# Expert loop with its tokens' rows loaded and turned inside the loop, 13 weight buffers, and two pairs' weights requested ahead of the router

## The chip, the cores and the metric

The kernel runs on one core of one Trainium2 chip. The metric is the device time of one execution in microseconds, taken as the median of several runs. Of the kernel before there are three: 3080.61, 3082.03 and 3091.97 us, median 3082.03.

## The reference

Two blocks are run one behind the other on 512 tokens of width 1024. The first has two layers, each a mixer (pooling and chunked attention in layer 0, a Mamba-2 mixer in layer 1) and behind it a mixture of experts; the second block is projections, retention, attention and convolutions over other inputs. The change is in the mixture of experts, which each layer runs once:

```python
def hier_moe(h, w_group, b_group, w_expert, b_expert, w1, w3, w2):
    ...
    g_prob = jax.nn.softmax(tf @ w_group + b_group, axis=-1)          # 4 groups
    g_val, g_idx = lax.top_k(g_prob, 1)
    e_logits = jnp.einsum('td,dge->tge', tf, w_expert) + b_expert      # 8 experts a group
    e_logits = e_logits[jnp.arange(b * s), g_idx[:, 0]]
    e_val, e_idx = lax.top_k(jax.nn.softmax(e_logits, axis=-1), MOE_TOP_K)   # 2
    e_val = e_val / jnp.sum(e_val, axis=-1, keepdims=True)
    weights = g_val * e_val
    expert_id = g_idx * MOE_EXPERTS_PER_GROUP + e_idx
    combine = jnp.sum(one_hot(expert_id, 32) * weights[..., None], axis=1)
    hid = jax.nn.silu(jnp.einsum('td,edf->tef', t, w1)) * jnp.einsum('td,edf->tef', t, w3)
    hid = hid * combine[:, :, None]
    y = jnp.einsum('tef,efd->td', hid, w2)
```

Each of the 512 tokens goes to 2 of 32 experts, so there are 1024 (token, expert) rows. An expert has 1024 x 256 weights for w1 and w3 and 128 x 1024 for w2, in float32.

## The kernel before

**The mixture of experts** is the method `moe` (L724). It normalizes the activations into `h2`, computes the router's 36 logits per token with TensorE (`pl`), and works out on VectorE which experts each token takes. The ranking matmuls `pk` (L822 to L826) count the rows in front of each row, and from them come `off` (where an expert's rows begin among the 1024), `cnt` (how many) and `pos` (each row's place). The activations are turned to token order (`pt`, tile `ht`) and GpSimd scatters them with eight indirect DMAs to their places in a buffer in memory, `dxs` (L855).

Then the rows are fetched. Eight DMAs (L872) read the 1024 rows back, 128 at a time, into `xr`; 64 transposes (`px`, in the helper `columns`, L1104) turn them, ScalarE and VectorE copy them from PSUM, and all of it stands in one large tile `xs`, with a column for each row.

The **expert loop** (`for q in range(17)`) takes two experts at a time, 64 rows each; its 17th pass is one extra block of 64 for an expert with more rows. For each pass `xc` receives the columns of the two experts from `xs`, at an offset read from a register, by a ScalarE and a GpSimd copy (L894, L892). `hidden` multiplies them with four weight tiles (`pa`, L906, a tile being 512 KB), and applies silu (`sl`, ScalarE) and the product (`hd`, VectorE). `turn` transposes the result (`ph`, then `hT` on ScalarE); `results` multiplies with two more weight tiles (`py`, L933), copies to `yrow` and scatters it to `dys` in memory (L935). `turn` and `results` of a pair come in the next pass. A pass requests its six weight tiles itself (`load`, L879), from a pool `pq` of 7 buffers. Behind the loop, `g` gathers each token's two rows from `dys` (L1008).

**Fills.** Work of the second block that needs nothing of the first is cut into pieces, which `fill(n)` puts between. A fill step is one 128 x 1024 weight tile: a 512 KB DMA into `stage` (L283), a split into a high part `whi` on ScalarE (L275) and a low part `wlo` on VectorE (L276), and 24 matmuls `mm` (L301) for one half of an output. Each second step ends with `out` on ScalarE and its 256 KB store `dpc` (L1947). The table `FILLS` says how many steps stand at each place; after each pair 0.7 in layer 0 and 1.0 in layer 1, and 10 and 16 in the router.

**Order.** A scheduler orders the instructions of each engine before the kernel runs, on its own estimates, under the dependencies of the tiles; on the chip an engine works its list in order. All weight, stage, row and store DMAs (but the scatters and gathers) are issued by SyncE (SP), one after the other, and a DMA that has to wait for its buffer holds back all that is behind it. In the router, `pstage` is a pool of 8 stage buffers of the method's own (`moes`).

Of the kernel before, what the change touches and what calls it, by code (L numbers as in the profile page):

```python
# [10 lines left out]
FT = mybir.dt.float32  # L11
# [7 lines left out]
ET = mybir.EngineType  # L19
# [180 lines left out]
SLOTS = 16  # L200

# [49 lines left out]
class K:  # L251
# [472 lines left out]
    def moe(self, l, fills, tail=None, norm=False):  # L724
# [8 lines left out]
        with ExitStack() as es:  # L733
# [3 lines left out]
            pt = pool("moet", ee, bufs=2)  # L737
# [4 lines left out]
            dxs, dys = (self.pdram.tile([D, D], FT, name=f"{n}{l}") for n in ("dxs", "dys"))  # L742
# [12 lines left out]
            nc.sync.dma_start(wr, I["router"][l].rearrange("p (k e) -> p k e", k=KT))  # L755
            pl = self.ps("a", "pl")
# [106 lines left out]
            self.pstage = stage  # L863
            eh.close()

            pe = pool("moee", ee, bufs=1)
# [10 lines left out]
            def load(src):  # L877
                w = pq.tile([P, D], FT, tag="w", name=self.n("w"))
                nc.sync.dma_start(w.rearrange("p (a f) -> p a f", a=src.shape[1]) if len(src.shape) == 3 else w, src)  # L879
                return w  # L880

            def place(ap):
                return nc.values_load(ap, engines=[ET.Pool, ET.Activation], min_val=0, max_val=D,
                                      skip_runtime_bounds_check_because="a place among 1024 pairs")

            def columns(places):

                xc = pq.tile([P, KT, 2, C], FT, tag="xc", name=self.n("xc"), bufs=2)
                for t, at in enumerate(places):
                    x = xs[:, :, ds(at, C)]  # L890
                    if t:
                        nc.gpsimd.tensor_copy(xc[:, :, t, :], x)  # L892
# [4 lines left out]
            def hidden(x, srcs, n):  # L897

                pa = self.ps("a", "pa")
                m = KT // len(srcs)  # L900
                for b, src in enumerate(srcs):
                    w = load(src)
                    for k in range(b * m, b * m + m):
                        for t in range(n):
                            c = t * 512 + (k - b * m) * 256
                            nc.tensor.matmul(pa[t * C:(t + 1) * C, :256], x[:, k, t, :], w[:, c:c + 256],  # L906
                                             start=(k == 0), stop=(k == KT - 1))
                    if b < len(srcs) - 1:
                        yield
# [5 lines left out]
                yield hd  # L915
# [9 lines left out]
            def results(w2, h, row):  # L925
# [3 lines left out]
                yr = pt.tile([P, D], FT, tag="row", name=self.n("yrow"), bufs=3)  # L929
# [10 lines left out]
            def slot(s, engines):  # L940
# [4 lines left out]
                srcs = [I["w13"][l, ds(e[0], 1), b * 2:b * 2 + 2, :, ds(e[1], 1), :].rearrange("o a p u f -> (o p) (a u) f") for b in range(2)]  # L945
                w2 = I["w2"][l, ds(e[0], 1), ds(e[1], 1)].rearrange("o u p f -> (o u p) f")
                return srcs, w2, [place(slots[0:1, 2, s])]
# [1274 lines left out]
```

## Time and profile before

| | before |
|---|---|
| median of 3 runs | 3082.03 us |
| the profiled execution, its own time | 3081.75 us |
| its span, first to last instruction | 3079.9 us |
| TensorE (PE) busy | 2857.2 us, 93% |
| VectorE (DVE) busy | 1889.4 us, 61% |
| ScalarE (ACT) busy | 1268.7 us, 41% |
| GpSimd (POOL) busy | 488.6 us, 16% |
| granted TensorE clock, mean | 0.967 |
| bytes moved by DMA | 503.74 MB, mean 164 GB/s |

Times in the profile count from the start of the span. A row of the timeline has start, duration, engine, line, operation, output and inputs, and how often it came in a row; in brackets stands the idle time before it and what ended it. PE is TensorE's matmuls, PEld its weight loads. The granted clock is 1.00 at 2.4 GHz and 0.50 at 1.2 GHz.

### The profile page before, as it was taken

How to read it: one execution, taken by the hardware profiler on the slowest of the kernel's cores; microseconds unless marked ns; L12 is line 12 of the kernel's file. 1: busy time of each engine (PE TensorE's matmuls, PEld its weight loads, DVE VectorE, ACT ScalarE, POOL GpSimd, SP SyncE). 2: the span in 40 equal slices, each digit the busy share in tenths (PEclk: the TensorE clock that was granted, in tenths of full speed). 3: DMA queues.
4: the chain of work that ended last, by engine and by line, in shares of the span. 5: the costliest groups of instructions: out<-in, count | busy, mean ns of one | idle time of the engine just before them, and what ended most of it. 6: DMA issues, size and time to landing. Idle time of an engine off the chain costs nothing.

```text
span 3079.9 us, 38679 instructions
## 1 busy us (share of the span) xinstructions
PE 2857.2 (93%) x14238; PEld 2167.4 (70%) x14238; DVE 1889.4 (61%) x3170; ACT 1268.7 (41%) x2006; POOL 488.6 (16%) x445
## 2 busy tenths in 40 slices
PE   7998878799999998888799999999999999999998
PEld 5566645677777785556687667777788766777887
DVE  7787311688989863116869754539645975453434
ACT  3445322455535452225553343344434344333424
POOL 0111110223303221101410000012111000001212
PEclk9999988899999999889999999999999999999999
DMA  8677988655542268886552222225544212222232
GB/s 294 220 238 266 329 331 289 202 169 166 164 147 65 91 236 305 314 290 205 182 180 85 62 68 83 93 93 179 192 129 139 87 60 67 82 93 79 89 96 82
DMA packets 174192, 503.74 MB, mean 164 GB/s; under 512 B 21936, under 2 KB 42032, under 8 KB 174000
## 3 DMA queue, kind: packets, MB, share of 16 engines
q1 hardware_dynamic: 164624, 476.07, 46.7%
q0 software_dynamic: 9376, 25.18, 2.2%
q8 instruction: 112, 1.84, 0.2%
q14 instruction: 80, 0.66, 0.1%
HBM read 464.07 MB, written 46.01 MB: 166 GB/s over the span
## 4 chain that ended last, share of the span: by engine, by line
PE 43%; DVE 4%; DMA 2%; issue 1%; ACT 1%; POOL 0%; DVEq 0%; SPq 0%; ACTq 0%; POOLq 0%
PE mm L301 34%; PE po L1508 1%; PE pp L1505 1%; DMA stage<-in_modT_dram 1%; DVE wlo L276 1%; PE po L1431 1%; PE st L1420 1%; PE as L1721 1%; PE as L1728 1%; PE pv L1617 0%; PE pv L1618 0%; DVE stage L337 0%; PE po L1442 0%; PE pv L1616 0%; DVE junk L337 0%
## 5 line engine op out<-in xcount | busy, mean ns | idle before, releaser
L301 PE MATMUL mm<-hhi,whi 128*128 128x512 f32 (+1 forms) x2488 | 943.2, 379 | 59.9 <-ACT whi L275 51.2
L301 PE MATMUL mm<-hhi,wlo 128*128 128x512 f32 (+1 forms) x2488 | 923.9, 371 | 8.0 <-DVE wlo L276 7.7
L301 PE MATMUL mm<-hlo,whi 128*128 128x512 f32 (+1 forms) x2488 | 919.4, 370 | 1.0 <-POOL hlo L393 1.0
L276 DVE TENSOR_TENSOR wlo<-stage,whi 128x1024 fp32r<-128x1024 f32 (+2 forms) x477 | 547.1, 1149 | 460.9 <-issue 193.1
L275 ACT ACTIVATE whi<-stage 128x1024 fp32r<-128x1024 f32 (+2 forms) x477 | 461.3, 968 | 822.2 <-PE mm L301 572.7
L301 PEld LDWEIGHTS mm<-hhi,whi 128*128 128x128 f32 x2488 | 485.3, 195 | 161.4 <-ACT whi L275 63.6
L301 PEld LDWEIGHTS mm<-hhi,wlo 128*128 128x128 f32 x2488 | 484.7, 195 | 104.9 <-issue 19.7
L301 PEld LDWEIGHTS mm<-hlo,whi 128*128 128x128 f32 x2488 | 484.4, 195 | 85.1 <-issue 17.5
L337 DVE SCALAR_TENSOR_TENSOR stage<-stage,row 128x1024 f32<-128x1024 f32 x160 | 209.3, 1318 | 21.3 <-DMA stage<-in_adaT_dram 15.3
L906 PE MATMUL pa<-w,xc 128*64 128x256 f32 x1056 | 165.5, 403 | 16.2 <-DMA w<-in_w_dram 16.1
L1633 DVE SCALAR_TENSOR_TENSOR cv<-cfu,cols,cv 128x512 f32<-128x512 f32 x240 | 171.7, 758 | 1.3
L1597 POOL TENSOR_TENSOR merged<-sig,merged 128x512 f32<-128x512 f32 x48 | 83.9, 1749 | 557.7 <-DVE sig L1596 548.5
L1102 DVE COPY yrow<-py 128x512 f32<-128x512 f32 (+1 forms) x34 | 23.5, 691 | 229.5 <-PE py L933 229.5
L301 PE MATMUL mm<-brh,whi 128*128 128x512 f32 (+1 forms) x384 | 142.1, 371 | 15.1 <-DVE merged L1594 5.8
L301 PE MATMUL mm<-brh,wlo 128*128 128x512 f32 (+1 forms) x384 | 141.7, 372 | 13.6 <-DVE wlo L276 13.3
L301 PE MATMUL mm<-brl,whi 128*128 128x512 f32 (+1 forms) x384 | 138.6, 361 | 0.5 <-DVE brl L276 0.4
L906 PEld LDWEIGHTS pa<-w,xc 128*64 128x64 f32 x1056 | 79.4, 140 | 80.5 <-issue 30.5
L301 PEld LDWEIGHTS mm<-brh,whi 128*128 128x128 f32 x384 | 74.8, 195 | 31.6 <-DVE merged L1594 6.6
L301 PEld LDWEIGHTS mm<-brh,wlo 128*128 128x128 f32 x384 | 74.1, 194 | 29.1 <-DVE wlo L276 17.6
L350 POOL TENSOR_TENSOR sqa<-sq,sqa 128x512 f32<-128x512 f32 (+1 forms) x44 | 59.9, 1360 | 176.9 <-ACT sq L352 172.4
L935 POOL DMA_INDIRECT dys<-yrow,ri x32 | 31.3, 978 | 345.8 <-DVE yrow L1102 232.3
L1372 ACT ACTIVATE att<-as,stat 128x512 f32<-128x512 f32 (+2 forms) x80 | 54.7, 687 | 70.0 <-DVE stat L1483 66.4
(477 smaller groups left out, 4279.3 us busy)
## 6 DMA issues: line engine op xcount, KB each, us to landing
stage<-in_winA_dram SPq DMA_DIRECT2D x252, 512.0 KB
w<-in_w_dram SPq DMA_DIRECT2D x198, 512.0 KB
stage<-in_adaT_dram SPq DMA_DIRECT2D x96, 512.0 KB
stage<-in_modT_dram SPq DMA_DIRECT2D x64, 512.0 KB
stage<-in_ssmA_dram SPq DMA_DIRECT2D x49, 512.0 KB
stage<-in_wbrA_dram SPq DMA_DIRECT2D x96, 256.0 KB
stage<-in_woutA_dram SPq DMA_DIRECT2D x24, 512.0 KB
dpc<-out SPq DMA_DIRECT2D x41, 256.0 KB
```

Source lines behind the costliest of these rows:

```text
L275: self.nc.scalar.activation(hi, src, AF.Copy)
L276: self.nc.vector.tensor_tensor(lo, src, hi.bitcast(FT), op=OP.subtract)
L301: nc.tensor.matmul(ps[:, po:po + n], w[:, k * P:(k + 1) * P], h[:, so:so + n], start=(k == first and w is hi and h is hh), stop=(k == last ...
L337: self.nc.vector.scalar_tensor_tensor(t if out is None else out, t, 1.0, vec, op0=OP.mult, op1=OP.mult, accum_out=acc)
L350: (engine or nc.gpsimd).tensor_tensor(self.sq_acc, self.sq_last, self.sq_acc, op=OP.add)
L906: nc.tensor.matmul(pa[t * C:(t + 1) * C, :256], x[:, k, t, :], w[:, c:c + 256], start=(k == 0), stop=(k == KT - 1))
L935: i = nc.gpsimd.indirect_dma_start(out=dys[:, :], out_offset=bass.IndirectOffsetOnAxis(ap=row, axis=0), in_=yr[r, :], in_offset=None, boun ...
L1372: self.nc.scalar.activation(out, in_, func, **kw)
L1420: nc.tensor.matmul(q["ps"][:, i, :T], kT[:, j * P:(j + 1) * P], qT, start=True, stop=True)
L1431: nc.tensor.matmul(q["po"][:, :T], v[j][:, h * P:(h + 1) * P], q[j], start=(j == 0), stop=(j == nt - 1 and cross is None))
L1597: nc.gpsimd.tensor_tensor(merged[f], sg, merged[f], op=OP.add)
L1633: nc.vector.scalar_tensor_tensor(c, u[:, t:t + T], self.col(f"cfw{l}_{t}", i), c, op0=OP.mult, op1=OP.add)
```

## The change

The large tile `xs` and its 64 transposes ahead of the loop go, as does the pool `moes`, so the router's fills use the ordinary stage pool of four buffers. The weight pool has 13 buffers, and the twelve tiles of the first two pairs are requested right behind the router's weights `wr`. In the loop, the rows of each pair come from `dxs` by two DMAs of 64 rows at an offset that SyncE reads into a register (`fetch_rows`), and eight transposes and two copies turn them (`columns`). Rows and weights of pair q + 2 are requested at the start of pass q. `dxs` gets 64 rows of zeros at its end, since an expert's 64 rows may reach beyond the 1024.

```diff
+WBUFS = 13
+AHEAD = 2
...
-            stage, self.pstage = self.pstage, pool("moes", eh, bufs=8)
+            dxs, dys = self.pdram.tile([D + C, D], FT, name=f"dxs{l}"), self.pdram.tile([D, D], FT, name=f"dys{l}")
+            zero = pht.tile([P, D], FT, tag="ht", name=self.n("zero"))
+            nc.gpsimd.memset(zero[0:C, :], 0.0)
+            nc.sync.dma_start(dxs[D:, :], zero[0:C, :])
...
+            def fetch(q):
+                return ([load(I["w13"][l, q, kk].rearrange("p t f -> p (t f)")) for kk in range(4)],
+                        [load(I["w2"][l, q, t]) for t in range(2)])
+            weights = [fetch(q) for q in range(AHEAD)]
             pl = self.ps("a", "pl")
...
-            pq = pool("moew", ee, bufs=7)
-            xs = pe.tile([P, KT, D + C], FT, name="xs")
-            nc.gpsimd.memset(xs[:, :, D:], 0.0)
-            for s in range(8):
-                xr = pt.tile([P, D], FT, tag="row", name=self.n("xr"), bufs=3)
-                nc.sync.dma_start(xr, dxs[s * P:(s + 1) * P, :])
-                self.columns(xr, lambda b: xs[:, b * 4:b * 4 + 4, s * P:(s + 1) * P])
...
+            def fetch_rows(places):
+                xr = pt.tile([P, D], FT, tag="row", name=self.n("xr"), bufs=3)
+                for t, ap in enumerate(places):
+                    at = nc.values_load(ap, engines=[ET.SP], min_val=0, max_val=D,
+                                        skip_runtime_bounds_check_because="a place among 1024 pairs")
+                    nc.sync.dma_start(xr[t * C:(t + 1) * C, :], dxs[ds(at, C), :])
+                return xr
+            def columns(xr, n):
+                r = slice(0, n * C)
+                xc = pt.tile([P, KT, P], FT, tag="xc", name=self.n("xc"), bufs=2)
+                for b in range(2):
+                    pp = self.ps("mm", "px", [P, 4, P])
+                    for k in range(4):
+                        nc.tensor.transpose(pp[:, k, r], xr[r, (b * 4 + k) * P:(b * 4 + k + 1) * P], ident[r, r])
+                    o = xc[:, b * 4:b * 4 + 4, r]
+                    if b:
+                        nc.vector.tensor_copy(o, pp[:, :, r])
                     else:
-                        nc.scalar.activation(xc[:, :, t, :], x, AF.Copy)
+                        nc.scalar.activation(o, pp[:, :, r], AF.Copy)
...
+            xr = [fetch_rows(place(q)) for q in range(AHEAD)]
             prev, wrote, owed = None, [], 0.0
-            x_ = columns(blocks[0][2]())
+            x_ = columns(xr[0], 2)
             for q in range(17):
+                if q + AHEAD < 16:
+                    xr.append(fetch_rows(place(q + AHEAD)))
+                    weights.append(fetch(q + AHEAD))
...
+                ws, w2 = weights[q]
+                x, n = x_, len(w2)
                 if q < 16:
+                    x_ = columns(xr[q + 1], len(weights[q + 1][1]) if q < 15 else 1)
+                if prev:
+                    hd = turn(prev[1], 2)
+                hd_ = hidden(x, ws, n)
+                if prev:
+                    wrote.append(results(prev[0], hd, prev[2]))
+                for _ in range(2):
+                    self.step()
                 owed += fills["pair"]
                 self.fill(int(owed))
```

The scheduler's order changes with it. On TensorE in layer 1's loop, this is what stood around one pair before: the last of a pair's hidden matmuls (`pa_10356`), a fill (`mm`), and the next pair's (`pa_10457`).

```order
L906 MATMUL pa_10356<-w_10391,xc_10254 64x256 x4
L906 MATMUL pa_10356<-w_10397,xc_10254 64x256 x4
L301 MATMUL mm_10314<-hhi_9078,whi_10415 128x256
L301 MATMUL mm_10314<-hlo_9079,whi_10415 128x256
L906 MATMUL pa_10457<-w_10458,xc_10353 64x256 x3
L301 MATMUL mm_10314<-hhi_9078,wlo_10416 128x256
```

The same place in the changed kernel, where the fill is L304, pa L916, ph L928:

```order
L916 MATMUL pa_10754<-w_10497,xc_10625 64x256 x4
L916 MATMUL pa_10754<-w_10499,xc_10625 64x256 x4
L916 MATMUL pa_10754<-w_10501,xc_10625 64x256 x4
L916 MATMUL pa_10754<-w_10503,xc_10625 64x256 x4
L928 MATMUL ph_10860<-cmt,hd_10773 128x128
L304 MATMUL mm_10573<-hhi_9160,whi_10576 128x256
L304 MATMUL mm_10573<-hlo_9161,whi_10576 128x256
L304 MATMUL mm_10573<-hhi_9160,wlo_10577 128x256
```

The turn `ph` of a pair has moved to right behind the pair's own hidden matmuls, and the fill's first matmul with `wlo` to right behind those with `whi`. Behind the 24 fill matmuls come the next pair's px (8), the py of the pair before, and the next pa. On ScalarE, the same stretch of layer 1 before (`xc` is the copy from `xs`, L883 its register load):

```order
L912 ACTIVATE sl_10504<-pa_10457 128x128
L883 TENSOR_LOAD offi
L894 ISA
L894 ACTIVATE xc_10559<-xs 128x8x64
L275 ACTIVATE whi_10523<-stage_10521 128x1024
L922 ACTIVATE hT_10571<-ph_10569 128x128
L1101 ACTIVATE yrow_10581<-py_10582 128x512
```

And now, where `xc` is the evacuation of px:

```order
L920 ACTIVATE sl_10771<-pa_10754 128x128
L930 ACTIVATE hT_10862<-ph_10860 128x128
L278 ACTIVATE whi_10576<-stage_10574 128x1024
L905 ACTIVATE xc_10737<-px_10738 128x512
L1101 ACTIVATE yrow_10775<-py_10776 128x512
```

So `whi` has moved from ahead of `hT` to behind it. At the head of layer 0's loop, TensorE before had the 64 px in groups of 8 or 16 between fill matmuls, beginning so:

```order
L1111 MATMUL px_2881<-cmt,xr_2879 128x128 x4
L1111 MATMUL px_2887<-cmt,xr_2879 128x128 x4
L1111 MATMUL px_2895<-cmt,xr_2893 128x128 x4
L1111 MATMUL px_2901<-cmt,xr_2893 128x128 x4
L301 MATMUL mm_3041<-hhi_2046,whi_3044 128x256
L301 MATMUL mm_3041<-hlo_2047,whi_3044 128x256
```

Now all 288 fill matmuls of the place stand ahead of the first px, and the first pair's pa right behind it:

```order
L304 MATMUL mm_2947<-hhi_2105,wlo_2981 128x256
L900 MATMUL px_3031<-cmt,xr_3011 128x128 x4
L900 MATMUL px_3037<-cmt,xr_3011 128x128 x4
L304 MATMUL mm_3169<-hhi_2046,whi_3172 128x256
L304 MATMUL mm_3169<-hlo_2047,whi_3172 128x256
L916 MATMUL pa_3077<-w_2380,xc_3030 64x256 x3
L900 MATMUL px_3065<-cmt,xr_3020 128x128 x4
L900 MATMUL px_3071<-cmt,xr_3020 128x128 x4
```

What has moved are 48 of the 64 transposes, from ahead of the loop into it, and 72 are new.

## Rows read from the trace of the kernel before

**Rows 1.** The page: busy time by engine, and the DMA issues of weights.

```profile
PE 2857.2 (93%) x14238; PEld 2167.4 (70%) x14238; DVE 1889.4 (61%) x3170; ACT 1268.7 (41%) x2006; POOL 488.6 (16%) x445
...
w<-in_w_dram SPq DMA_DIRECT2D x198, 512.0 KB
```

**Rows 2.** Windows: us; PE, PEld, DVE, ACT, POOL busy; clock; DMA share; GB/s.

```profile
338.90:522.10 183.20, 147.21 (x892) 88.52 (x894) 32.74 (x63) 40.93 (x77) 23.88 (x30) 0.91 0.87 324
1175.00:1369.50 194.50, 163.83 (x1003) 104.53 (x1003) 35.68 (x59) 44.09 (x81) 22.43 (x29) 0.89 0.84 309
360.00:380.00 20.00, 14.74 (x86) 7.07 (x83) 1.96 (x4) 3.57 (x8) 3.20 (x4) 0.91 0.95 358
1090.00:1115.00 25.00, 24.17 (x144) 16.85 (x145) 16.80 (x50) 15.97 (x24) 1.62 (x2) 1.00 0.26 76
1143.00:1160.00 17.00, 16.10 (x134) 15.48 (x132) 8.04 (x8) 7.70 (x10) 0.51 (x1) 1.00 0.82 282
```

**Rows 3.** Waits of PE, us, times, longest: first 1118 to 1395, then 298 to 545.

```profile
PE mm L301 <- ACT whi L275: 31.0, 14, 2.8
...
PE pa L906 <- DMA w<-in_w_dram: 1.9, 3, 1.3
...
PE mm L301 <- ACT whi L275: 20.2, 9, 2.5
PE pa L906 <- DMA w<-in_w_dram: 14.2, 15, 2.2
```

**Rows 4.** Timeline of PE, one pair of layer 1.

```profile
1248.60 1.90 PE L906 MATMUL pa<-w,xc 128*64 128x256 f32 x16
1252.65 0.38 PE L301 MATMUL mm<-hhi,whi 128*128 128x256 f32 x1 [2.16 <-ACT whi L275]
...
1260.16 1.89 PE L933 MATMUL py<-w,hT 128*64 128x512 f32 x8
1261.88 1.90 PE L906 MATMUL pa<-w,xc 128*64 128x256 f32 x16
...
1268.19 0.41 PE L301 MATMUL mm<-hhi,wlo 128*128 128x256 f32 x1
1268.40 0.41 PE L301 MATMUL mm<-hhi,whi 128*128 128x256 f32 x1
```

**Rows 5.** Timeline of ACT, the same pair.

```profile
1250.54 0.28 ACT L912 ACTIVATE sl<-pa 128x128 f32<-128x128 f32 x1 [1.96 <-PE pa L906]
1251.02 0.63 ACT L894 ACTIVATE xc<-xs 128x512 f32 x1 [0.21 <-ACT sl L912]
1251.56 1.04 ACT L275 ACTIVATE whi<-stage 128x1024 fp32r<-128x1024 f32 x1
```

**Rows 6.** Timeline of DVE, the same pair.

```profile
1252.63 1.23 DVE L276 TENSOR_TENSOR wlo<-stage,whi 128x1024 fp32r<-128x1024 f32 x1 [1.49 <-ACT whi L275]
```

**Rows 7.** Windows of 2 us, the same pair; columns as in rows 2.

```profile
1251.00:1253.00 2.00, 0.35 (x2) 0.30 (x2) 0.51 (x2) 1.58 (x2) 0.89 (x2) 1.00 1.02 391
1253.00:1255.00 2.00, 2.00 (x11) 1.09 (x10) 0.86 (x1) 0.00 (x0) 0.00 (x0) 0.68 0.97 379
...
1257.00:1259.00 2.00, 2.00 (x15) 1.48 (x14) 0.00 (x0) 0.48 (x1) 0.00 (x0) 0.96 0.14 57
```

**Rows 8.** Line L822: ns min/median/max, first and last start, forms.

```profile
L822 PE MATMUL pk<-ob,ltb x8: 176/176/177, 297.4 to 1118.4; 128*128 128x32 bf16 x8
```

**Rows 9.** Line L906, both layers; columns as in rows 8.

```profile
L906 PE MATMUL pa<-w,xc x1056: 379/379/690, 342.9 to 1381.4; 128*64 128x256 f32 x176
```

**Rows 10.** Timeline of PE, the head of layer 1's loop.

```profile
1159.99 1.06 PE L1111 MATMUL px<-cmt,xr 128*128 128x128 f32 x8 [0.85 <-DMA xr<-dxs]
...
1174.85 1.46 PE L906 MATMUL pa<-w,xc 128*64 128x256 f32 x10
```

**Rows 11.** Timeline of PE, the last result matmuls of layers 0 and 1.

```profile
536.81 1.93 PE L933 MATMUL py<-w,hT 128*64 128x512 f32 x4
...
1388.40 1.93 PE L933 MATMUL py<-w,hT 128*64 128x512 f32 x4
```

More of the change, by code (lines that the diff above doesn't have):

```diff
@@ L874, in moe @@
             rows, slots, srow = self.blocks(pt, off, cnt)
             self.fill(fills["columns"])
[L877 to L884, printed above, removed]
@@ L893, in columns, with hidden @@
                     else:
-                        nc.scalar.activation(xc[:, :, t, :], x, AF.Copy)
+                        nc.scalar.activation(o, pp[:, :, r], AF.Copy)
                 return xc
-            def hidden(x, srcs, n):
+            def hidden(x, ws, n):
                 pa = self.ps("a", "pa")
-                m = KT // len(srcs)
-                for b, src in enumerate(srcs):
-                    w = load(src)
+                m = KT // len(ws)
+                for b, w in enumerate(ws):
@@ L928, in results @@
                 r = slice(0, n * C)
-                yr = pt.tile([P, D], FT, tag="row", name=self.n("yrow"), bufs=3)
+                yr = pt.tile([P, D], FT, tag="yrow", name=self.n("yrow"), bufs=2)
                 for b in range(2):
@@ L938, in results, with slot @@
                 return i.ins
-            def slot(s, engines):
+            def slot(s):
+                xr = fetch_rows([slots[0:1, 2, s]])
                 e = [nc.values_load(slots[0:1, j, s], engines=[ET.SP], min_val=0, max_val=m,
@@ L944, in slot @@
                      for j, m in enumerate((15, 1))]
-                srcs = [I["w13"][l, ds(e[0], 1), b * 2:b * 2 + 2, :, ds(e[1], 1), :].rearrange("o a p u f -> (o p) (a u) f") for b in range(2)]
-                w2 = I["w2"][l, ds(e[0], 1), ds(e[1], 1)].rearrange("o u p f -> (o u p) f")
-                return srcs, w2, [place(slots[0:1, 2, s])]
-            blocks = []
-            for q in range(16):
-                srcs = [I["w13"][l, q, kk].rearrange("p t f -> p (t f)") for kk in range(4)]
-                w2s = [I["w2"][l, q, t] for t in range(2)]
-                blocks.append((srcs, w2s, functools.partial(lambda q: [place(offi[0:1, 2 * q + t:2 * q + t + 1]) for t in range(2)], q), rows[:, q:q + 1]))
+                ws = [load(I["w13"][l, ds(e[0], 1), b * 2:b * 2 + 2, :, ds(e[1], 1), :].rearrange("o a p u f -> (o p) (a u) f")) for b in range(2)]
@@ L954, in moe @@
+                return xr, (ws, [load(I["w2"][l, ds(e[0], 1), ds(e[1], 1)].rearrange("o u p f -> (o u p) f"))])
+            place = lambda q: [offi[0:1, 2 * q + t:2 * q + t + 1] for t in range(2)]
+            xr = [fetch_rows(place(q)) for q in range(AHEAD)]
             prev, wrote, owed = None, [], 0.0
-            x_ = columns(blocks[0][2]())
+            x_ = columns(xr[0], 2)
             for q in range(17):
-                if q < 16:
-                    srcs, w2s, _, row = blocks[q]
-                else:
-                    srcs, w2, _ = last
-                    w2s, row = [w2], srow[0:C, 0:1]
-                x = x_
-                if q < 15:
-                    x_ = columns(blocks[q + 1][2]())
-                elif q == 15:
-                    last = slot(slice(0, 1), None)
-                    x_ = columns(last[2])
-                h = hidden(x, srcs, len(w2s))
-                ws = []
-                for b in range(len(srcs)):
-                    hd_ = next(h)
-                    if b % 2 == len(w2s) - 1 or len(srcs) == 2 and b == 0:
-                        ws.append(load(w2s[len(ws)]))
-                    if prev and b == 0:
-                        hd = turn(prev[1], len(prev[0]))
-                    if prev and b == 1:
-                        wrote.append(results(prev[0], hd, prev[2]))
-                    if b % 2:
-                        self.step()
@@ L982, in moe @@
                 owed -= int(owed)
-                prev = ws, hd_, row
+                prev = w2, hd_, rows[:, q:q + 1] if q < 16 else srow[0:C, 0:1]
             wrote.append(results(prev[0], turn(prev[1], 1), prev[2]))
```

41 lines of the change are left out of this document (15 added, 26 removed).

## The prediction, made before the changed kernel was run

> **What bounds the kernel now.** TensorE is busy for 93% of the span [rows 1], so time can only come from stretches where it waits or runs slow; the change touches two, the expert loops of the two layers. I read those first by stretch [rows 2], then by what TensorE waits for [rows 3], then one pair of experts on three engines [rows 4 to 6].
>
> The loop runs from 342.9 us to about 538.7 in layer 0 and from 1174.85 to about 1390.3 in layer 1 (first hidden matmul [rows 9, 10], end of the last result matmuls [rows 11]). There the granted clock is 0.91 and 0.89, the DMA share 0.87 and 0.84 [rows 2]. It looks like a loop held by its weights, 512 KB each [rows 1]. The waits say otherwise, in layer 1 most clearly: 31.0 us go to `whi`, ScalarE's half of a split fill weight, and 1.9 to an expert weight. In layer 0 it is 20.2 against 14.2 [rows 3].
>
> One pair of layer 1 shows why. Sixteen hidden matmuls start at 1248.60, the next such sixteen at 1261.88: a cycle of 13.28 us. When they end (1250.50), ScalarE does `sl`, the copy `xc` and only then `whi`, so TensorE stands for 2.16 us [rows 4, 5]. Then the clock falls: 0.68 from 1253 to 1255, back at 0.96 from 1257 to 1259 [rows 7]. Fill matmuls start 0.21 us apart at the low level (1.2 GHz) [rows 4], 0.12 at the high one (2.4 GHz): 17 us hold 134 starts with px among them [rows 2]. Such a pause costs its length and about 1.6 us more.
>
> **The change part by part.**
>
> *The head of the loop gets shorter.* Before, 64 px transposes and their waits stand between ranking and first pair. After, only two pairs' rows (16 transposes) do, and 12 weights are requested before the router; ahead of layer 1's ranking the DMA engines are 26% busy [rows 2], so the weights are free there. In layer 0 the ranking matmuls start at 297.4 [rows 8]; the order has 288 fill matmuls behind them, 288 x 0.12 = 34.6, and 2 x 1.06 of px [rows 10]: first pair at about 334.5 instead of 342.9, **-8**. Layer 1: 1118.4 + 343 x 0.12 = 1159.6, and 2.1: about 1162 instead of 1174.85, **-13**.
>
> *Bytes.* A pair's rows now come from memory as they are used, with padding: 17 blocks, 8.65 MB a layer against 8 x 0.524 = 4.2 before. A pair with a fill tile moves 6 x 0.524 (weights) + 0.52 (rows) + about 0.26 (results) + 0.52 (stage) + 0.13 (half a dpc) = 4.5 MB. At 358 GB/s, the rate of 20 well-filled us [rows 2], 12.6 us; at 379 [rows 7], 11.9.
>
> [...]
>
> *Transposes.* 72 more per layer in the loop, 8 to a pair at 1.06 us [rows 10], all on TensorE. The runtime-offset copies on ScalarE and GpSimd go, and an `xc` evacuation on ScalarE and VectorE comes for each. Both lie under the 1.89 us of py that now stand between px and pa [rows 4], so I cost them at nothing; without that cover it would be about 0.7 a pair.
>
> *The order in the pair, the term that matters.* In the new order ph stands directly behind its own pair's sixteen pa, then 24 fills, px, py of the pair before, and pa. On ScalarE `whi` is behind `hT`, so the fill waits for a chain: sl 0.28, hd and hT (same size, taken as 0.28), whi 1.04 [rows 5], and its third matmul for wlo 1.23 [rows 6]. With gaps as in those rows: sl ends 0.32 after pa, hd 0.64, ph 1.0, hT 1.4, whi 2.4, wlo 3.7. Before, six pa matmuls covered wlo and the fill covered sl to ph. So from pa's end to the third fill matmul 3.7 us pass, in which TensorE does ph and two fill matmuls. With the clock as after the 2.16 us pause: 22 fills, 17 x 0.21 + 5 x 0.12 = 4.2. Cycle: 3.7 + 4.2 + 1.0 (px) + 1.75 (py) + 3.7 (pa) = **14.3 us**, where it was 13.28. The waits of a pair without fill are shorter; its work is 7.5 us, and there the weights set the pace, about 12.4.
>
> The unknown in it is the clock. If it stays high, 22 x 0.12 = 2.6 and the cycle is 12.7, about the DMA's own 12.6. If it stays low until pa: fills 22 x 0.21 = 4.6, px and py not faster than twice their 2.75, so up to 2.8 more, 17.4. I take 14.3, as the rows show the clock back some 3.5 us after it fell.
>
> *SyncE* issues two loads of a register and two DMAs for each pair's rows ahead of six weights. In both kernels it stands in line for buffers anyway; with 13 of them a wait of a `dpc` is no longer ahead of the next pair's weights but of those two pairs on. I cost it at nothing, up to 1 us a pair (16 each layer) if it were late.
>
> *Sum.* Layer 0: until pair 6 the loop is held by bytes: 30 weights, 7 pairs' rows, two stages, results and dpc, 22 MB from 334.5, at 358 GB/s to 396. Then the order has seven filled pairs and two without up to pair 15, 7 x 14.3 + 2 x 10 = 120, 516; a last cycle for the extra block, 530 against 538.7: **-9**. Layer 1: pair 4 ends at about 1199 (14 MB from 1160); then 12 cycles of 14.3, 1371, and 8 to 9 for the last ph, fill and py: 1379.5 against 1390.3: **-11**. So most of the 21 us won at the heads stays, and the longer cycle takes back what 13 buffers give. Behind the loops the fills, TensorE-bound, are the same. The profiled execution took 3081.75 us (span 3079.9), 0.28 under the median: 3082 - 20 = **3062 us**.
>
> **The rivals.**
>
> A, *as forecast*, 3062, own range 3050 to 3076 (a cycle of 13.6 to 15.0 on 19 filled pairs, 19 x 0.7 = 13 each way). Chance 0.47.
>
> B, *the clock stays high*; the loops are then held by bytes: the cycle is 12.7 to 12.9, 19 x 1.45 = 28 better, 3034. For it: clock 1.00 from 1143 to 1160, where TensorE works with short pauses only [rows 2]. Against: the pause grows from 2.16 to about 3, and after the shorter one the clock fell. Between A and B lie mixtures. Chance 0.14.
>
> C, *the head is not shorter, or the requests ahead do nothing*: stage loads of the router's fills queue behind 12 weights (6.3 MB, 17.6 us at 358) with four stage buffers where eight were, and the fills start that much late, in layer 0 above all. Each us is one of TensorE's. The 21 us go and 3083 is left. For it: the DMA engines are 87% busy in layer 0's loop already, so nothing is given away. Against: layer 1's request falls into free time [rows 2]. Chance 0.21.
>
> D, *slower: the clock stays low through the rest of the pair.* TensorE's pause at sl, hT, whi, wlo is then followed by fills, px and py at 1.2 GHz; the cycle becomes 16.5, and 19 x 2.2 = 42 us come on top of A: 3104. It turns slower than before from a cycle of 15.4 (19 x 1.1 = 21). For it: twice as many links in the chain as before, and 0.68 after the short one. Against: it recovered within the cycle [rows 7]. [...] Chance 0.18.
>
> **How the numbers follow.** The likeliest is A. Within 0.5% (15 us, about what can be told from no change) means 3067 to 3097. Faster: two thirds of A (0.32), all of B, some of C (0.05): 0.51. Same: the rest of A and most of C: 0.31. Slower: D: 0.18. The range reaches to B's 3034 and most of the way to D: 3036 to 3100.
>
> **What would show it.** First pa at about 334 and 1162. In layer 1's loop a wait of fills for `whi` and `wlo` of some 2.3 us a pair, one of ph for `hd` of 0.7, the copies `xc<-xs` gone, a clock near 0.88 and a DMA share near 0.9 early and 0.85 late. A clock over 0.95 there says B, under 0.8 D; stage tiles late behind weights between 290 and 330 say C. A loop whose TensorE waits mainly for `w` would make the cycle argument wrong.

## The result, and the profile after

The changed kernel takes 3121.9 us (median of 4 runs, 3117.2 to 3125.5) against 3083.4 us of the kernel before beside it: ratio 1.0119, 95% interval 1.0094 to 1.0144. It is slower by 38 us. The forecast was 3062, and its range ended at 3100. The profiled execution took 3123.2 us, its span is 3121.4.

The page of the changed kernel, TensorE's row and the bytes (503.74 MB before); then the two loops as windows, in the columns of [rows 2]:

```profile
PE 2871.6 (92%) x14382; PEld 2198.0 (70%) x14382; DVE 1904.4 (61%) x3188; ACT 1258.4 (40%) x1989; POOL 470.5 (15%) x413
...
DMA packets 177331, 513.22 MB, mean 164 GB/s; under 512 B 22768, under 2 KB 42864, under 8 KB 177136
```

```profile
335.90:544.40 208.50, 165.04 (x1023) 108.21 (x1022) 38.14 (x59) 41.02 (x82) 16.09 (x16) 0.86 0.91 306
1178.60:1425.70 247.10, 194.01 (x1218) 138.64 (x1217) 48.67 (x67) 52.12 (x95) 16.03 (x16) 0.85 0.82 279
```

The kernel before, over its own loops in the same view:

```profile
342.90:538.70 195.80, 157.98 (x927) 93.78 (x926) 34.88 (x63) 45.18 (x84) 24.20 (x31) 0.90 0.87 320
1174.90:1390.30 215.40, 181.78 (x1096) 116.55 (x1095) 41.76 (x66) 51.54 (x93) 24.35 (x30) 0.90 0.83 303
```

The reader is to see three things. Both loops are longer, by 12.7 and 31.7 us; the clock is lower; and at about the same DMA share fewer bytes move. GB/s divided by the share is what the DMA engines move when all are busy: 368 and 365 before, 336 and 340 after. This quotient is called the **full-share rate** below.

The heads of the loops, as ranking and first hidden matmuls (columns of [rows 8]; for L839 [rows 8] has 297.4 and 1118.4, for pa [rows 9] has 342.9 and [rows 10] 1174.85):

```profile
L839 PE MATMUL pk<-ob,ltb x8: 176/184/188, 295.2 to 1131.5; 128*128 128x32 bf16 x8
...
L916 PE MATMUL pa<-w,xc x1056: 378/379/634, 335.9 to 1410.9; 128*64 128x256 f32 x176
```

The first pair of layer 0 starts 7.0 us earlier. In layer 1 the way from ranking to first pair is 47.1 us (1131.5 to 1178.6), where it was 56.5. The rest is lost. The spans add up so: head -7.0, loop of layer 0 +12.7, from there to the ranking of layer 1 +7.4 (49 more fill matmuls stand between that loop and the same point behind it, 310 against 261), head of layer 1 -9.4, its loop +31.7, behind it +6.1: 41.5, which is 3121.4 - 3079.9.

What TensorE waits for, layer 1's loop (1178 to 1425) and then layer 0's with its head (298 to 560), in the view of [rows 3]:

```profile
PE mm L304 <- ACT whi L278: 33.2, 12, 5.1
PE ph L928 <- DVE hd L922: 8.4, 12, 0.7
PE mm L304 <- DVE wlo L279: 6.4, 11, 0.8
PE py L941 <- ACT xc L905: 3.4, 12, 0.3
PE px L900 <- DMA xr<-dxs: 1.5, 1, 1.5
...
PE mm L304 <- ACT whi L278: 18.0, 9, 4.5
PE px L900 <- DMA xr<-dxs: 12.6, 6, 3.4
```

No expert weight is waited for any more in layer 1. One pair shows the chain that the prediction had added up (timeline of TensorE, as [rows 4]); behind the "..." in the middle stand the next pair's rows:

```profile
1276.31 3.62 PE L916 MATMUL pa<-w,xc 128*64 128x256 f32 x32
1280.64 0.33 PE L928 MATMUL ph<-cmt,hd 128*128 128x128 f32 x1 [0.70 <-DVE hd L922]
1282.34 0.39 PE L304 MATMUL mm<-hhi,whi 128*128 128x256 f32 x1 [1.37 <-ACT whi L278]
...
1283.60 0.39 PE L304 MATMUL mm<-hhi,wlo 128*128 128x256 f32 x1 [0.76 <-DVE wlo L279]
...
1290.92 3.62 PE L916 MATMUL pa<-w,xc 128*64 128x256 f32 x32
1295.25 0.33 PE L928 MATMUL ph<-cmt,hd 128*128 128x128 f32 x1 [0.70 <-DVE hd L922]
1300.71 0.58 PE L304 MATMUL mm<-hhi,whi 128*128 128x256 f32 x1 [5.13 <-ACT whi L278]
```

From 1276.31 to 1290.92 is 14.6 us; 14.3 was forecast. The next pair takes 17.9, since its fill stands 5.13 us for `whi`. ScalarE's and the DMA queue's timelines say why:

```profile
1281.23 1.05 ACT L278 ACTIVATE whi<-stage 128x1024 fp32r<-128x1024 f32 x1
...
1299.60 1.06 ACT L278 ACTIVATE whi<-stage 128x1024 fp32r<-128x1024 f32 x1 [3.64 <-DMA stage<-in_winA_dram]
```

```profile
1270.83 2.79 SPq L764 DMA_DIRECT2D w<-in_w_dram  x3
1288.64 0.33 SPq L1936 DMA_DIRECT2D dpc<-out  x1
1289.06 1.35 SPq L764 DMA_DIRECT2D w<-in_w_dram  x3
1290.51 0.38 SPq L286 DMA_DIRECT2D stage<-in_winA_dram  x1
1291.39 1.44 SPq L891 DMA_DIRECT2D xr<-dxs  x2
1292.93 7.04 SPq L764 DMA_DIRECT2D w<-in_w_dram  x6
```

After the first three weights SyncE issues nothing from 1273.6 to 1288.64: it stands before the store of `dpc`, whose tile `out` ScalarE writes only when the fill is done. Only then come three weights and the stage tile of the next fill. Requested at 1290.51, it is in time for nothing: ScalarE has it at 1299.60. Such stands sum to 85.8 us in seven pieces, the longest 15.1:

```profile
SPq L1936 <- ACT out L1361: 85.8, 7, 15.1
```

The kernel before stands for the same store (63.6 us in eight pieces from 1175 to 1390, the longest 10.2), and there too the stage tile is asked for behind it, but one weight behind, and in time. Asked for at 1260.04, it is used at 1264.85 without a wait:

```profile
1259.14 0.33 SPq L1947 DMA_DIRECT2D dpc<-out  x1
1259.57 0.37 SPq L879 DMA_DIRECT2D w<-in_w_dram  x1
1260.04 0.40 SPq L283 DMA_DIRECT2D stage<-in_winA_dram  x1
...
1264.85 1.04 ACT L275 ACTIVATE whi<-stage 128x1024 fp32r<-128x1024 f32 x1
```

So 4.8 us from request to use were enough before, and 9.1 us went by in the changed kernel, where three weights stand ahead of the tile and rows and six weights close behind it. ScalarE's waits for stage tiles, before (1179 to 1370) and after (1210 to 1420):

```profile
ACT whi L275 <- DMA stage<-in_winA_dram: 0.7, 2, 0.5
ACT whi L278 <- DMA stage<-in_winA_dram: 15.9, 8, 3.6
```

So every other pair is late: twelve cycles of layer 1 alternate between 14.6 to 16.4 and 16.7 to 18.0 us, 16.4 in the mean.

### The profile page after: what moved, and what is told of

The parts are those of the page before. It is cut to its first block, busy times and chain, and to the rows that moved or that the text cites. A ratio compares the mean times of both kernels' runs of the same rounds, so it can differ in the third digit from the quotient of the medians.

```text
span 3121.4 us, 39028 instructions
## 1 busy us (share of the span) xinstructions
PE 2871.6 (92%) x14382; PEld 2198.0 (70%) x14382; DVE 1904.4 (61%) x3188; ACT 1258.4 (40%) x1989; POOL 470.5 (15%) x413
## 4 chain that ended last, share of the span: by engine, by line
PE 44%; DVE 4%; issue 1%; ACT 1%; DMA 1%; POOL 0%; DVEq 0%; ACTq 0%; POOLq 0%
PE mm L304 35%; PE po L1497 1%; PE pp L1494 1%; DVE wlo L279 1%; PE po L1420 1%; PE st L1409 1%; PE as L1710 1%; DMA stage<-in_modT_dram 1%; DVE stage L340 1%; PE as L1717 0%; PE pv L1606 0%; PE pv L1607 0%; PE pv L1605 0%; PE po L1431 0%; DVE junk L340 0%
## 5 line engine op out<-in xcount | busy, mean ns | idle before, releaser
L304 PE MATMUL mm<-hhi,whi 128*128 128x512 f32 (+1 forms) x2488 | 951.0, 383 | 61.1 <-ACT whi L278 52.7
L304 PE MATMUL mm<-hhi,wlo 128*128 128x512 f32 (+1 forms) x2488 | 931.9, 375 | 20.1 <-DVE wlo L279 19.7
L304 PE MATMUL mm<-hlo,whi 128*128 128x512 f32 (+1 forms) x2488 | 927.4, 373 | 1.5 <-POOL hlo L396 1.3
L304 PEld LDWEIGHTS mm<-hhi,whi 128*128 128x128 f32 x2488 | 492.2, 198 | 157.6 <-ACT whi L278 58.5
L304 PEld LDWEIGHTS mm<-hhi,wlo 128*128 128x128 f32 x2488 | 492.0, 198 | 113.1 <-DVE wlo L279 31.8
L304 PEld LDWEIGHTS mm<-hlo,whi 128*128 128x128 f32 x2488 | 492.9, 198 | 85.1 <-issue 16.6
L304 PE MATMUL mm<-brh,whi 128*128 128x512 f32 (+1 forms) x384 | 142.4, 371 | 13.5 <-DVE merged L1583 5.8
L304 PE MATMUL mm<-brh,wlo 128*128 128x512 f32 (+1 forms) x384 | 141.8, 372 | 12.9 <-DVE wlo L279 12.6
L304 PE MATMUL mm<-brl,whi 128*128 128x512 f32 (+1 forms) x384 | 139.0, 362 | 0.1
L916 PE MATMUL pa<-w,xc 128*64 128x256 f32 x1056 | 126.3, 381 | 0.2 <-issue 0.2
L903 DVE COPY xc<-px 128x512 f32<-128x512 f32 (+1 forms) x34 | 23.0, 675 | 157.8 <-PE px L900 157.8
L916 PEld LDWEIGHTS pa<-w,xc 128*64 128x64 f32 x1056 | 77.7, 138 | 52.8 <-issue 17.7
L304 PEld LDWEIGHTS mm<-brh,whi 128*128 128x128 f32 x384 | 74.6, 194 | 29.2 <-DVE merged L1583 6.6
L304 PEld LDWEIGHTS mm<-brh,wlo 128*128 128x128 f32 x384 | 74.2, 194 | 28.5 <-DVE wlo L279 16.7
L304 PEld LDWEIGHTS mm<-brl,whi 128*128 128x128 f32 x384 | 74.9, 195 | 9.7 <-issue 0.5
```

The lines of the kernel that those rows point to most:

```text
L304: nc.tensor.matmul(ps[:, po:po + n], w[:, k * P:(k + 1) * P], h[:, so:so + n], start=(k == first and w is hi and h is hh), stop=(k == last ...
L916: nc.tensor.matmul(pa[t * C:(t + 1) * C, :256], x[:, k, t * C:(t + 1) * C], w[:, c:c + 256], start=(k == 0), stop=(k == KT - 1))
```

## The experiments

Three theories stood at first, with the letters of the recorded expectations: Q, SyncE's stand before the `dpc` store makes the next stage tile late; S, the chain that TensorE waits for before a fill and the clock after it; B, the bytes of the rows. Two came up on the way: R, the offsets in registers; P, the rows' pieces cover only 64 partitions. Medians are given with that of the kernel before beside them only where it matters; ratios are to that kernel, with the 95% interval. Windows and waits are of the one execution that was profiled: it took 3112 us in run 1, 3109 in run 9, 3148 in run 10 and 3010 in run 11, so there the loops and the medians do not add up exactly.

**1. The store on another queue.**

```diff
-            nc.sync.dma_start(self.dpc[i], o.rearrange("p j t -> p (j t)"))
+            nc.scalar.dma_start(self.dpc[i], o.rearrange("p j t -> p (j t)"))
```

> The changed kernel (3122 us) with one edit: the dpc stores are issued by ScalarE behind the out that they store, not by SyncE. Theory Q (SyncE stands for a dpc, up to 15 us, and the next fill's stage tile behind it comes late, so whi waits 2.7 to 5.1 us in every other pair instead of 1.37): the late pairs go to the 14.6 us of the others, 12 x 1.8 in layer 1 and 8 x 1 in layer 0, 30 us less, 3092. Theory S (the chain sl, hd, ph, hT, whi, wlo on TensorE's path and the clock behind it are all of the loss): 3117 to 3124. Theory B (the padded rows' bytes): 3122.

3101.3 us, ratio 1.0046 (1.0028 to 1.0064): 20 us back. The loops take 197.9 and 231.4 us.

```profile
344.40:542.30 197.90, 162.03 (x1020) 102.45 (x1020) 37.68 (x58) 39.61 (x81) 16.10 (x16) 0.87 0.95 317
1181.10:1412.50 231.40, 190.70 (x1213) 134.21 (x1212) 47.39 (x66) 49.28 (x92) 15.98 (x16) 0.88 0.89 294
```

The share is up, the full-share rate is not (334, 330). TensorE's waits for `whi` in layer 1's loop fall from 33.2 us in 12 pieces to 16.5 in 10. Q is real, two thirds of the 30 us that it expected and about half of the loss. How much of the 20 us is the queue alone is not shown: the scheduler's order moves with the edit (the first pair starts at 344.4 us, not 335.9), and the same edit was not tried on the kernel before.

**2. The chain interleaved with the next pair's hidden matmuls.** `hidden` yields before its last part; the turn and the results of the pair before go there.

```diff
+                h = hidden(x, ws, n)
+                for b in range(len(ws)):
+                    hd_ = next(h)
+                    if prev and b == 0:
+                        hd = turn(prev[1], 2)
+                    if prev and b == 1:
+                        wrote.append(results(prev[0], hd, prev[2]))
```

> The changed kernel with turn and results of a pair issued inside the next pair's hidden matmuls, as before the change; rows, buffers and requests stay. The order then has ph after four of the next pair's matmuls and whi directly behind sl. Theory S: the pause before a fill loses the wait of ph for hd (0.70) and ph and hT ahead of whi (about 0.4): 1.1 a pair on some 19 to 20 pairs with a fill, 21 us less, 3101. Theories Q and B: 3122, since neither the queue nor the bytes change.

3115.9, ratio 1.0108 (1.0077 to 1.0138): 6 us of the 21 that S expected. Waits for `hd` go, and those for `whi` grow from 33.2 to 39.3 us in layer 1, because its stage tile is late all the same. This way of removing the pause missed.

**3. Rows loaded for the first two pairs only.**

```diff
-                    xr.append(fetch_rows(place(q + AHEAD)))
+                    xr.append(xr[q])
```

> The changed kernel, but the rows of pairs 2 to 15 are not loaded: the first two pairs' tiles are used over again (this leaves out the loads of the other rows). 28 DMAs of 256 KB and their register loads are gone per layer, 7.3 MB, all transposes stay. Theory B: 7.3 MB at 358 GB/s is 20 us a layer, 40 in all, 3082. Theories S and Q: only the waits of px for rows in layer 0 go (12.6 us in 6 waits), 3108 to 3115.

3020.8, ratio 0.9788 (0.9754 to 0.9822): 101 us less, more than any theory expected, where the bytes as such (7.3 MB a layer, 19 us each at 380 GB/s) were worth 38 at most. The full-share rate is 389 and 376. The order of the instructions differs too, so this only says where to look: at the row loads, beyond their bytes.

**4. No fills in the loops.**

```diff
-columns=2, pair=0.7
+columns=13, pair=0.0
...
-columns=2, pair=1.0
+columns=19, pair=0.0
```

> The changed kernel with the loop's fill steps (11 in layer 0, 17 in layer 1) moved ahead of the loop. Theories S and Q: a pair without fill is held by its bytes, 3.9 MB or 11 us, against 16.4 measured with a fill in layer 1 and some 15 in layer 0; 12 x 5.4 + 8 x 4 = 97 less, and 28 fills x 2.9 = 81 more ahead of the loops: 3106, and no wait for whi in the loop. Theory B (the loop is held by bytes, fills are free in it): 81 more, 3200.

3127.5, ratio 1.0145 (1.0111 to 1.0179), between the two expectations. The fills done elsewhere cost about what the loops save, so the total says little. The loops say much:

```profile
368.80:557.70 188.90, 136.98 (x801) 72.95 (x800) 28.95 (x51) 30.28 (x70) 15.01 (x16) 0.82 0.98 309
1236.90:1431.50 194.60, 147.65 (x915) 85.26 (x914) 32.66 (x54) 33.44 (x74) 16.09 (x16) 0.83 1.00 302
```

All DMA engines are busy and move 302 to 309 GB/s; without the rows they moved 376 to 389 for a full share. The loop is held by its transfers at a rate well under the 358 of the prediction.

**5. The same rows on 128 partitions.** Each piece of 64 rows is loaded as 128 half rows of 2 KB; four transposes and one rearranging copy a piece give the same `xc`.

```diff
-                    nc.sync.dma_start(xr[t * C:(t + 1) * C, :], dxs[ds(at, C), :])
+                    nc.sync.dma_start(xr[:, t * 512:(t + 1) * 512], dxs[ds(at, C), :].rearrange("r (h f) -> (r h) f", h=2))
...
+                        nc.tensor.transpose(pp[:, k, :], xr[:, t * 512 + k * P:t * 512 + (k + 1) * P], ident)
```

> The changed kernel, but the 64 rows of an expert are loaded onto 128 partitions, half a row on each (2 KB packets); four transposes of 128 x 128 turn a piece and its copy puts the halves apart. Bytes, register loads and DMA count stay, and ph, hT, whi stay one behind the other. Theory P (a load into 64 partitions slows what moves beside it: without fills, run 4, the DMA share was 1.00 at 302 GB/s, with the rows loaded only for two pairs, run 3, 0.86 at 323): share times rate as in run 3, the late stage tiles and the waits for rows go, 12 x 1.8 in layer 1 and some 20 us in layer 0, 3080. Theory R (the register offset of the row loads) and theory S (the chain alone): 3115 to 3125.

3068.9, ratio 0.9939 (0.9916 to 0.9963): 53 us back with the same bytes, DMA count and offsets.

```profile
346.00:530.10 184.10, 153.53 (x1008) 98.22 (x1007) 37.17 (x57) 38.57 (x80) 16.10 (x16) 0.90 0.88 338
1164.50:1374.80 210.30, 181.68 (x1211) 127.81 (x1210) 46.69 (x65) 50.01 (x93) 16.04 (x16) 0.90 0.85 320
```

The full-share rate is 384 and 376. P holds; R and S, which expected 3115 and more, do not explain it. The order of instructions moved as well (9 waits for `whi` in layer 1, not 12), so not all of the 53 us need be the rate.

**6. Rows at constant places.**

```diff
-                    nc.sync.dma_start(xr[t * C:(t + 1) * C, :], dxs[ds(at, C), :])
+                    nc.sync.dma_start(xr[t * C:(t + 1) * C, :], dxs[len(xrs) * 31 + t * 32:len(xrs) * 31 + t * 32 + C, :])
```

> The changed kernel, but the rows are loaded from constant places (pair q from row 31 q and 31 q + 32; this leaves out the true places); the register loads stay, and so do 64 partitions, bytes and the order on TensorE and ScalarE. Theory R: the weights move at full rate again, 3080. Theories P and S: 3115 to 3125.

3121.1, ratio 1.0125 (1.0106 to 1.0145), full-share rate 338 and 340: as the changed kernel, with the same order of instructions. R falls.

**7 and 8. The fill's weights split early**, on the changed kernel and on the one before: stage, `whi` and `wlo` of the next fill are requested at the top of the pass.

```diff
+    def prep(self):
+        if self.nxt is None and self.coming is not None:
+            with self.tc.high_priority():
+                self.nxt = self.weight(self.I["winA"][0, self.coming])
...
             for q in range(17):
+                if q < 16 and owed + fills["pair"] >= 1.0:
+                    self.prep()
```

> The changed kernel with the stage load and the split of each fill's weights requested a pass ahead and given a higher priority in the scheduler, so whi and wlo are there before ph. Theory S: the waits for whi (51 us), wlo (11) and the low clock behind them go, 3072. Theory P: the DMA engines are full then; run 4's loops, 195 and 189 us, plus 17 and 11 fill tiles of 0.65 MB at 302 GB/s are 231 and 212 against 247 and 208 now, so 3106.

> The kernel before (3084 us) with the same edit of the fills' weights. Theory S: TensorE waited 51 us for whi in its loops, and about 1.6 us more a pause went to the clock; held by bytes at 342 to 358 GB/s then, 24 us less in layer 1 and 12 in layer 0, 3047. If the pauses are covered by the DMA engines anyway: 3084.

On the changed kernel 3092.6, 1.0023 (1.0006 to 1.0041): 29 us less, between S and P. On the one before 3053.3, 0.9892 (0.9865 to 0.9919): 32 less. So asking early for the fill's weights is worth about 30 us in both kernels and doesn't tell them apart. What is left of the changed kernel waits for rows (18.7 us in layer 1):

```profile
PE px L900 <- DMA xr<-dxs: 18.7, 8, 4.0
```

**9. Rows on every other partition**: the first piece of a pair onto the even, the second onto the odd partitions, the copies rearrange. Every instruction stands where it does in the changed kernel.

```diff
-                    nc.sync.dma_start(xr[t * C:(t + 1) * C, :], dxs[ds(at, C), :])
+                    nc.sync.dma_start(xr[t::2, :] if len(places) == 2 else xr[:C, :], dxs[ds(at, C), :])
```

> The changed kernel with one edit: a pair's two pieces of 64 rows are loaded onto the even and the odd partitions, not onto the lower and the upper half; the copy from PSUM puts the columns apart again. Bytes, packets of 4 KB, DMA count, places and the order of TensorE and ScalarE are the same. Theory P1 (a load onto one contiguous half of the partitions is what slows the others): as with the rows on 128 partitions in run 5, less what its order gave, 3070 to 3095. Theory P2 (any load of 64 packets onto 64 partitions does): 3115 to 3125.

3100.2, ratio 1.0055 (1.0033 to 1.0076): 22 us back, between the two expectations. The full-share rate is 387 and 378:

```profile
337.50:532.00 194.50, 159.78 (x1022) 105.07 (x1022) 38.52 (x60) 41.05 (x82) 16.11 (x16) 0.89 0.85 329
1172.40:1412.50 240.10, 195.66 (x1218) 139.82 (x1217) 48.67 (x67) 51.42 (x94) 16.03 (x16) 0.85 0.76 287
```

The rate is whole again, and SyncE stands before the store as long as ever (85.8 us in layer 1, the longest 15.3). So the contiguous half costs the rate, and 22 us: the loops are 14.0 and 7.0 us shorter. That what is left is Q is argued here; run 14 tests it.

**10 and 13. The same on the kernel before.** Its `w2` tiles of 16 pairs are loaded as two DMAs of 64 partitions, not a byte more: lower and upper half (10), even and odd (13). The diff is that of 10; in 13 the `for` line has `slice(0, P, 2), slice(1, P, 2)`, and nothing else differs.

```diff
+                if halves:
+                    for r in (slice(0, C), slice(C, P)):
+                        nc.sync.dma_start(w[r, :], src[r, :])
+                    return w
```

> The kernel before with each w2 tile of the 16 pairs requested as two DMAs of 64 partitions, the lower and the upper half (32 tiles a layer, twice the row pieces that the change loads). No byte more, no other edit. Theory P1: packets over 250 ns rise from 5% to 15% or more, the DMA share of the loops goes from 0.83 to 0.87 towards 1.00 at some 300 GB/s, 15 to 40 us more, 3100 to 3125. Were it the rows' extra bytes or their place in memory instead: 3084.

> The kernel before, its `w2` tiles again loaded as two DMAs of 64 partitions, but onto the even and the odd partitions instead of the lower and the upper half. Instructions, their order, DMA count and bytes are those of the run with halves (3157). Theory P (what costs is that a transfer stays on one contiguous half): 3083 to 3100, and the loops move bytes at 365 GB/s or more for each full share, as before, against 296 to 303 with halves. Theory N (twice as many DMAs of half the size cost it): 3145 to 3165, at about 300.

With halves 3156.6, ratio 1.0249 (1.0210 to 1.0288); on every other partition 3130.5, 1.0139 (1.0122 to 1.0156). The full-share rates are 302 and 303 against 367 and 360. First the run with halves, then the one on every other partition:

```profile
347.00:575.80 228.80, 168.36 (x930) 98.78 (x929) 33.50 (x59) 44.22 (x83) 24.28 (x30) 0.85 0.91 275
1209.20:1455.30 246.10, 193.37 (x1096) 125.07 (x1096) 43.21 (x70) 53.13 (x94) 25.97 (x31) 0.85 0.89 270
```

```profile
345.10:555.00 209.90, 160.83 (x930) 97.07 (x929) 34.87 (x63) 45.41 (x84) 24.70 (x31) 0.89 0.82 301
1187.00:1439.70 252.70, 194.90 (x1096) 127.91 (x1095) 43.27 (x69) 53.14 (x94) 26.02 (x31) 0.84 0.73 263
```

Both theories are half right. The contiguous half costs the rate and some 26 us (the four executions with halves lie between 3148 and 3170, and of the two loops only layer 0's is longer with them). Another 45 us come with splitting each tile into two DMAs, which also moves a few instructions against the kernel before, at a low share (0.73) and with long waits in layer 1:

```profile
PE mm L301 <- ACT whi L275: 52.8, 14, 4.8
```

In [rows 3] these are 31.0 us, in as many pieces. SyncE stands before the store for 67.5 us in this loop, against 63.6 before, so that alone does not make the difference. What in the splitting makes `whi` late (SyncE's issues, the landing of two transfers) wasn't tried.

**11 and 12. Rows on 128 partitions with early fill weights**, and with the store on ScalarE as well (edits of 5, 7 and 1).

> The changed kernel with both edits, rows on 128 partitions (run 5, 3069) and the fills' weights early (run 7, 29 us less; on the kernel before, run 8, 32 less). The DMA engines at full rate and no wait for whi (35 us in run 5's loops) nor the low clock behind: 3069 - 30 = 3039. If the two edits gain the same time: 3065.

> As run 11, and the dpc stores issued by ScalarE as in run 1 (20 us less there). Where SyncE's wait for out still holds back weights: 3030. If the early fills have taken that wait away: as run 11, 3039.

3020.8, ratio 0.9794 (0.9774 to 0.9814), and 3024.4, 0.9803 (0.9782 to 0.9824). The first is the fastest version of all, 63 us under the kernel before; the store's queue adds nothing once the stage tile is asked for early. The two edits together give 101 us, more than their sum of 82; that is not explained by a run of its own. The loops of run 11:

```profile
337.80:507.40 169.60, 152.70 (x1058) 94.16 (x1057) 38.19 (x58) 40.02 (x80) 15.62 (x16) 0.98 0.96 372
1133.70:1314.70 181.00, 163.48 (x1174) 108.13 (x1173) 44.08 (x63) 45.45 (x88) 15.61 (x16) 0.99 0.95 367
```

**14 and 15. Every other partition, with the store on ScalarE, and with early fill weights** (edits of 9 and 1, of 9 and 7).

> The changed kernel, rows on every other partition, and the store of `dpc` issued by ScalarE. Rows on every other partition alone gave 3100, with full rate for each share (378 to 384 GB/s) but a share of only 0.76 to 0.85 and SyncE standing 86 us for `out` in layer 1's loop. Theory W (what is left there is SyncE's wait, which makes every other stage tile late): 3068 to 3082. Theory H (a transfer on 64 partitions costs something else as well, whichever they are): 3092 to 3102.

> The changed kernel, rows on every other partition, and the fill weights split at the top of the pass. Theory W: as the run with rows on 128 partitions and early fill weights, 3020 to 3040, at 375 GB/s or more for each full share. Theory H: 3055 to 3075, between that and early fill weights alone (3093).

With the store moved 3079.6, ratio 0.9976 (0.9963 to 0.9990); with early weights 3044.9, 0.9867 (0.9851 to 0.9884). The first is what W said: 22 us (run 9) and 20 us (run 1) add up to the 42 that it is under the changed kernel, and the whole loss against the kernel before is gone. Runs 1 and 14, and runs 7 and 15, are two more pairs that have every instruction in the same place and differ only in the partitions: 22 and 48 us, so the contiguous half costs more once the stage tiles are asked for early. The second lies between W and H: 24 us above run 11, so every other partition is not quite as good as 128 there, or the other order costs it; that stays open.

```profile
339.20:523.00 183.80, 154.23 (x1020) 98.84 (x1019) 37.67 (x58) 39.55 (x81) 16.10 (x16) 0.91 0.89 341
1162.30:1382.50 220.20, 188.06 (x1213) 132.32 (x1212) 47.37 (x66) 49.14 (x92) 15.98 (x16) 0.88 0.83 307
```

## Why the prediction was wrong

**The heads**: right in sign and nearly in size. First pair at 335.9 (334.5 forecast), and 9.4 us won in layer 1 where 13 were forecast.

**The chain and the cycle**: the chain was right, the cycle only where the stage tile is there. 14.6 us measured for 14.3, `hd` 0.70, `whi` 1.37, `wlo` 0.76, and the third fill matmul 3.67 us after the end of pa for 3.7. As a mean the cycle is wrong, and this is the term of the sum that failed. The loops, cut where the forecast cut them (end of pair 6's pa and of pair 15's in layer 0, of pair 4's pa and twelve cycles on in layer 1):

```profile
335.90:396.80 60.90, 52.48 (x365) 31.84 (x364) 9.85 (x18) 11.57 (x25) 4.90 (x5) 0.92 1.01 329
396.80:532.40 135.60, 101.94 (x609) 71.35 (x609) 23.60 (x34) 24.38 (x46) 8.76 (x9) 0.82 0.90 303
1178.60:1213.40 34.80, 33.25 (x259) 21.59 (x258) 7.21 (x12) 7.29 (x17) 2.95 (x3) 1.00 0.92 325
1213.40:1410.70 197.30, 145.76 (x861) 105.68 (x862) 36.81 (x50) 38.16 (x68) 12.10 (x12) 0.81 0.81 277
```

The forecast had 61.5, 120, 37 and 171.6 us. The two stretches that go by the cycle lose 15.6 and 25.7 us; ahead of them it is a little less than forecast, and the ends of the loops together take 27.0 us for 22.5. The cycle takes for granted that stage tile and rows have landed when they are needed; two premises behind that failed.

**"Bytes ... At 358 GB/s"**: the first premise that failed. The rate came from stretches [rows 2, 7] in which every large transfer went to 128 partitions, and was put on one in which a ninth of the bytes goes to 64. The full-share rate fell from 366 to 338, and runs 9, 10, 13, 14 and 15 show that it is the contiguous half of the partitions that lowers it; run 9 measures 22 us. How slow the rows themselves went can be estimated from layer 1's loop, for no view shows their rate by itself: at a share of 0.82 its 247.1 us are worth 202.6 us of full engines. All but the 7.6 MB of rows, 61.3 of its 68.9 MB, take 162.3 us of that at the 378 GB/s of run 9; that leaves 40.3 us for the rows, 188 GB/s, half the rate of the rest. On every other partition the rate is whole: 387 and 378 in run 9, and 367 and 360 in run 13 against 368 and 365 in the kernel before. A pair's terms add up to 4.6 MB, not 4.5; at 338 GB/s that is 13.6 us, still under 14.3, so the rate does not set the pace by its mean. It makes late what is waited for after a stand of SyncE; that is argued, the 22 us are measured. That the stretch held by bytes came out (60.9 us for 61.5) is luck: 20.0 MB moved at 329 GB/s, not 22 at 358. For two us at a time the engines move more than the 391 and 379 of [rows 7]: run 13 has 420 GB/s at a share of 1.04 from 1264 to 1266.

**"SyncE ... I cost it at nothing"**: the second. The prediction saw that the `dpc` wait now stands elsewhere in the queue, named a price of up to 16 us a layer and gave it no chance. It did not see that the next fill's stage tile, one weight behind the store before, now stands behind three. Run 1 measures 20 us, with what its order of instructions gives; run 14, with rows and store both changed, takes 3079.6 us. No run changes the 13 buffers or the requests two pairs ahead by themselves; with them and without the later rows (run 3) the kernel takes 3020.8.

**"Behind the loops the fills ... are the same"**: a smaller step that failed. In the changed kernel the stretch between the loops and the one behind them are 7.4 and 6.1 us longer than before. In run 14 both loops together take 404.0 us, 413 were forecast (195.5 and 217.5), and yet it is 18 us over the forecast: the stretch between the loops is 639.3 us (1162.3 - 523.0) against 623 by the forecast's terms, and behind layer 1's loop it is 8.6 more than before. Part of it is fill work that no longer lies in the loop, 49 matmuls in the changed kernel; what the rest is stays open.

**The rivals.** D gave 3104, by cycles of 16.5 us with the clock low to the end of the pair. The mean came out at that length mostly for another reason, so the agreement is luck: in the late pair shown the clock is back within the fill (fill matmuls 0.12 us apart from 1304.44 on), and the time is lost before the first fill matmul. D has a part in it: in five of the twelve cycles the clock is still low at px, which then takes 1.21 to 1.58 us for 1.04. The two levels of the clock, which the prediction gives in GHz, can be read from the trace of before only as rates of columns, an estimate: 128x256 fill matmuls start 0.213 us apart at a granted clock of 0.50 (1255 to 1257), which is 1.2 columns a ns; at 1.00 they start 0.120 apart (1143 to 1147) and 128x512 ones 0.227 (2300 to 2304), so 256 more columns take 0.107 us, 2.4 columns a ns. C's late stage tiles came too, but in the loop behind the store, not in the router behind weights. B fell: over the twelve cycles the granted clock is 0.81.

## What to carry to other kernels

Before a tile is loaded in pieces, look at which partitions each piece covers: moving the rows from halves to even and odd partitions gave 22 us here with every instruction in its place, and half rows on 128 partitions 53, some of it perhaps by another order. Take a transfer rate only from a stretch with transfers of the same shape, and read GB/s and DMA share together; their quotient showed the slow transfer here (368 and 365 before, 336 and 340 after) where the share, 0.87 and 0.83 against 0.91 and 0.82, did not. Where a store waits on a queue for work of this pass, list what stands behind it for the next.

## What the runs showed of the hardware that was not expected

- Loads onto a contiguous half of the partitions lower what busy DMA engines move: 302 and 303 GB/s with a quarter of the bytes in halves (run 10: 15 to 16 MB of 62.9 and 66.4), 336 to 340 with a ninth (changed kernel), 376 to 388 with none (runs 5, 11); on even or odd partitions 360 to 387 (runs 9, 13, 14, 15).
- With the engines nearly never idle the loss is larger than the half rate estimated above explains: 315 and 302 GB/s in run 4, where 13% of the bytes in halves at that rate would give 378 / 1.13 = 335. Why is open.
- A core's DMA engines moved 367 and 372 GB/s over whole loops of 181 and 170 us (run 11), above the 358 that the prediction took.
- The pause before a fill (2.16 us in [rows 4], with the clock at 0.50 from 1255 to 1257 after it) can be taken out by asking for the fill's weights at the top of the pass. TensorE's waits for `whi` in the two loops go from 18.0 and 33.2 us to none in run 7, and from 20.2 and 31.0 to 1.3 and 1.0 in run 8; the granted clock goes from 0.86 and 0.85 to 0.87 and 0.91, and from 0.90 and 0.90 to 0.93 and 0.94; 29 and 32 us were won.
